# A batched matrix product on one core: the first y ahead of the first x in the load queue

## The chip, the cores and the metric

The kernel runs on one core of a Trainium2 chip. The metric is the device time of one execution in microseconds (us). The time before is the median of eight runs.

## The reference

`x` is (32, 256, 512) and `y` is (32, 512, 384), both float32. For each of the 32 batches the result is the matrix product of the two, (256, 384), float32:

```
def reference(x, y):
    return np.einsum('bij,bjk->bik', x, y).astype(np.float32)
```

16.8 MB of x and 25.2 MB of y are read, and 12.6 MB of output are written. Each is moved once.

## The kernel before

The work goes in pairs of batches (`G = 2`), 16 pairs in all (`U`). x is loaded for four batches at once (`Q = 4`) by `load_x(q)` at L66: one transfer of 2048 KB, in which each of the 128 partitions gets one contiguous run of 16 KB. y is loaded one batch at a time at L81: a transfer of 768 KB, 6 KB for each partition. A pair's output is stored by one transfer of 768 KB at L150. All these transfers are issued by SyncE, on one queue.

TensorE contracts over partitions, so x has to be turned around first. `transpose(q, half)` does it with 16 TensorE transposes of 128 x 128 in float32 (L99) into PSUM tiles `t_ps`, four transposes to a tile. VectorE (L105) and ScalarE (L107) take turns in copying these to `xt_sb` as float16. `round_y(u)` casts a pair's y to float16 in eight pieces of 128 x 384, four on ScalarE (L116) and four on VectorE (L118). `multiply(u)` runs 32 matmuls (L130) into four PSUM tiles `o_ps`; `collect(u)` copies these to `o_sb` on ScalarE (L143) and VectorE (L145); `store(u)` issues the output's transfer.

Nothing is left to a scheduler: `keep` fixes the order in which each engine meets its instructions to the order of the program. Two pairs are loaded ahead (`ahead`), and then the loop over `s` loads pair `s + 2`, collects pair `s - 2`, multiplies pair `s - 1`, rounds pair `s`, transposes a half of the next x where one is due, and stores pair `s - 2`. In step 0 both halves of the first x are transposed ahead of the first rounding. `load(u)` puts the next x in front of its own two y for every second pair, so that the queue of SyncE begins with x 0, two y of pair 0, x 1, two y of pair 1, two y of pair 2, x 2. The first store stands on that queue behind the loads of pairs 0 to 4.

There are three buffers for x, five pairs of y, two of rounded y, two of turned x and five of output. PSUM is shared half and half by transposes (four tiles) and matmuls (four tiles).

Of the kernel before, what the change touches and what calls it, by code (L numbers as in the profile page):

```python
# [1 line left out]

# [5 lines left out]


MM_DT = mybir.dt.float16  # L10
F32 = mybir.dt.float32
P = 128


Q = 4
G = 2

LAG = 4


@with_exitstack
def kernel(
    ctx: ExitStack,
    tc: tile.TileContext,
    x: bass.AP,
    y: bass.AP,
    out: bass.AP,
):
    nc = tc.nc

    B, I, J = x.shape
    _, _, K = y.shape


    M = P // G
    NE = I // M
    NJ = J // P

    PQ = P // Q
    R = I // PQ
    H = R // NE
    U = B // G

    const_pool = ctx.enter_context(tc.tile_pool(name="const", bufs=1))
    x_pool = ctx.enter_context(tc.tile_pool(name="x_pool", bufs=3))
    y_pool = ctx.enter_context(tc.tile_pool(name="y_pool", bufs=5))
    yr_pool = ctx.enter_context(tc.tile_pool(name="yr_pool", bufs=2))
    xt_pool = ctx.enter_context(tc.tile_pool(name="xt_pool", bufs=2))  # L50
    o_pool = ctx.enter_context(tc.tile_pool(name="o_pool", bufs=5))
    tpsum_pool = ctx.enter_context(tc.tile_pool(name="tpsum", bufs=4, space=bass.MemoryType.PSUM))
    opsum_pool = ctx.enter_context(tc.tile_pool(name="opsum", bufs=4, space=bass.MemoryType.PSUM))


    keep = tc.keep_in_program_order

    identity = const_pool.tile([P, P], F32)
    make_identity(nc, identity)

    x_of, y_of, yr_of, xt_of, ps_of, o_of = {}, {}, {}, {}, {}, {}

    def load_x(q):
        x_of[q] = x_pool.tile([P, R, J], F32, name="x_sb")
        keep(
            nc.sync.dma_start(  # L66
                out=x_of[q],
                in_=x[q * Q : (q + 1) * Q].rearrange("g (p r) j -> (g p) r j", r=R),
            )
        )  # L70

    def load(u):

        if u == 0:
            load_x(0)
        if (u + 1) * G % Q == 0 and u + 1 < U:
            load_x((u + 1) * G // Q)
        y_of[u] = y_pool.tile([P, G, NJ, K], F32, name="y_sb")
        for g in range(G):
            keep(  # L80
                nc.sync.dma_start(  # L81
                    out=y_of[u][:, g],
                    in_=y[u * G + g].rearrange("(q t) k -> q t k", q=P),
                )
            )

    def transpose(q, half):

        x_sb = x_of[q]
        if half == 0:  # L90
            xt_of[q] = xt_pool.tile([P, NJ, NE, Q * PQ, H], MM_DT, name="xt_sb")
        n = 0
        for t in range(half * NJ // 2, (half + 1) * NJ // 2):
            for e in range(0, NE, 2):
                t_ps = tpsum_pool.tile([P, 2, H, Q * PQ], F32, name="t_ps")
                for f in range(2):
                    for h in range(H):
                        keep(
                            nc.tensor.transpose(  # L99
                                t_ps[:, f, h], x_sb[:, h * NE + e + f, t::NJ], identity  # L100
                            )
                        )
                dst = xt_of[q][:, t, e : e + 2].rearrange("c f p h -> c f h p")
                if n % 2 == 0:
                    keep(nc.vector.tensor_copy(dst, t_ps))  # L105
                else:
                    keep(nc.scalar.copy(dst, t_ps))  # L107
                n += 1

    def round_y(u):  # L110
        y_sb = y_of.pop(u)
        yr_of[u] = yr_pool.tile([P, G, NJ, K], MM_DT, name="y_r")
        for g in range(G):
            for t in range(NJ):
                if t % 2 == 0:
                    keep(nc.scalar.copy(yr_of[u][:, g, t], y_sb[:, g, t]))  # L116
                else:
                    keep(nc.vector.tensor_copy(yr_of[u][:, g, t], y_sb[:, g, t]))  # L118

    def multiply(u):  # L120
        xt_sb, y_r = xt_of[u * G // Q], yr_of.pop(u)
        ps_of[u] = []
        for e in range(NE):
            o_ps = opsum_pool.tile([P, K], F32, name="o_ps")
            ps_of[u].append(o_ps)
            for t in range(NJ):
                for g in range(G):
                    a = (u * G + g) % Q
                    keep(
                        nc.tensor.matmul(  # L130
                            o_ps[g * M : (g + 1) * M],
                            xt_sb[:, t, e, a * PQ : (a + 1) * PQ].rearrange("c p h -> c (p h)"),
                            y_r[:, g, t],
                            start=(t == 0),
                            stop=(t == NJ - 1),
                        )
                    )

    def collect(u):
        o_of[u] = o_pool.tile([P, NE, K], F32, name="o_sb")  # L140
        for e in range(NE):
            if e % 2 == 0:
                keep(nc.scalar.copy(o_of[u][:, e], ps_of[u][e]))  # L143
            else:
                keep(nc.vector.tensor_copy(o_of[u][:, e], ps_of[u][e]))  # L145
        del ps_of[u]

    def store(u):
        keep(
            nc.sync.dma_start(  # L150
                out=out[u * G : (u + 1) * G].rearrange("g (m e) k -> (g m) e k", e=NE),
                in_=o_of.pop(u),
            )
        )


    ahead = LAG - 2
    for u in range(ahead):
        load(u)
    for s in range(U + 2):  # L160
        if s + ahead < U:
            load(s + ahead)
        if s == 0:
            transpose(0, 0)
            transpose(0, 1)
        if s >= 2:
            collect(s - 2)
        if 1 <= s <= U:
            multiply(s - 1)
        if s < U:  # L170
            round_y(s)
        for half in range(2):
            q = (s + 1 - half) * G // Q
            if (s + 1 - half) * G % Q == 0 and 0 < q < B // Q:
                transpose(q, half)
        if s >= 2:
            store(s - 2)


# [1 line left out]
_INS = ['x', 'y']  # L181
_OUTS = [((32, 256, 384), 'float32')]


# [23 lines left out]
```

## Time and profile before

| What | Value |
|---|---|
| median of 8 runs | 136.1 us (135.97 to 136.31) |
| the profiled execution | 136.31 us |
| its span, first to last instruction | 134.4 us |
| TensorE matmul busy | 91.9 us (68%) |
| VectorE, ScalarE busy | 56.5 us (42%), 64.0 us (48%) |
| DMA queue of the kernel | 54.53 MB, 97.7% of the 16 engines' span |
| mean rate | 406 GB/s over the span |
| mean granted TensorE clock | 0.909 |

The span is shorter than the execution by 1.9 us, which lie around it. Busy times are sums over an engine's instructions. A line such as "y_r L116 <- DMA y_sb" in the waits means that the instruction of line 116 could start when that transfer had landed. "SPq" is the queue of SyncE: an instruction that waits there holds up all that is behind it. In the timeline, what stands in square brackets is the idle time ahead of an instruction and what ended it. An answer by windows has, for each stretch of time, the busy time of each engine, the granted TensorE clock, the busy share of the DMA engines and the rate that they reached.

### The profile page before, as it was taken

To read this page: it belongs to the slowest core of one execution; us is meant where nothing else is said; L and a number is where in the kernel's file an instruction comes from. 1 tells how busy PE (TensorE), PEld (TensorE's weight loads), DVE (VectorE), ACT (ScalarE), POOL (GpSimd) and SP (SyncE) were. 2 spreads that over 40 slices of the span, in tenths; PEclk is the share of its full clock that TensorE was granted. 3 is DMA by queue.
4 is the path that set the end of the run, shared out by engine and by line. 5 is a ranking of instruction groups with operands and counts; after the bars stand their busy time and mean duration, and the time that the engine had idled before them with its cause. 6 is when DMAs were issued, how large, how long until landed. Compare 5 with 4: busy or idle time off the path is not lost.

```text
span 134.4 us, 1968 instructions
## 1 busy us (share of the span) xinstructions
PE 91.9 (68%) x768; PEld 75.2 (56%) x768; DVE 56.5 (42%) x128; ACT 64.0 (48%) x129; POOL 0.7 (1%) x6
## 2 busy tenths in 40 slices
PE   0049599688697925979089780997929793597920
PEld 0049568576586824768067660776726683466810
DVE  0014614744747056261644418324273704628520
ACT  3004744935766067361754428425385505737710
POOL 2000000000000000000000000000000000000000
PEclk9999968999999997799977997569986999869999
DMA  5999999999999999999999999999999999999993
GB/s 107 429 402 451 409 417 417 459 386 426 409 451 410 411 422 419 461 388 425 418 436 450 395 422 422 449 427 397 419 426 455 403 413 428 420 428 419 414 375 145
DMA packets 8073, 54.65 MB, mean 406 GB/s; under 512 B 896, under 2 KB 896, under 8 KB 7040
## 3 DMA queue, kind: packets, MB, share of 16 engines
q1 hardware_dynamic: 8064, 54.53, 97.7%
q8 instruction: 6, 0.10, 0.3%
q14 instruction: 3, 0.02, 0.0%
HBM read 41.94 MB, written 12.58 MB: 406 GB/s over the span
## 4 chain that ended last, share of the span: by engine, by line
DMA 78%; PE 13%; ACT 4%; DVE 0%; issue 0%
DMA y_sb<-in_y_dram 40%; DMA x_sb<-in_x_dram 38%; PE o_ps L130 11%; ACT xt_sb L107 2%; PE t_ps L99 2%; ACT y_r L116 1%; ACT o_sb L143 1%; DVE o_sb L145 0%
## 5 line engine op out<-in xcount | busy, mean ns | idle before, releaser
L130 PE MATMUL o_ps<-y_r,xt_sb 128*64 128x384 f16 x512 | 55.5, 379 | 28.1 <-ACT o_sb L143 20.3
L130 PEld LDWEIGHTS <-xt_sb 128*64 128x64 f16 x512 | 40.6, 126 | 39.3 <-issue 22.0
L116 ACT CAST y_r<-y_sb 128x384 f16<-128x384 f32 x64 | 29.4, 513 | 36.3 <-DMA y_sb<-in_y_dram 36.3
L99 PE MATMUL t_ps<-identity,x_sb 128*128 128x128 f32 x256 | 37.4, 304 | 8.7 <-DMA x_sb<-in_x_dram 8.6
L99 PEld LDWEIGHTS t_ps<-identity,x_sb 128*128 128x128 f32 x256 | 34.6, 212 | 13.8 <-issue 13.3
L118 DVE CAST y_r<-y_sb 128x384 f16<-128x384 f32 x64 | 19.9, 355 | 43.8 <-DMA y_sb<-in_y_dram 43.8
L107 ACT CAST xt_sb<-t_ps 128x512 f16<-128x512 f32 x32 | 22.6, 732 | 26.2 <-PE t_ps L99 26.2
L105 DVE CAST xt_sb<-t_ps 128x512 f16<-128x512 f32 x32 | 22.7, 730 | 26.9 <-PE t_ps L99 26.9
L145 DVE COPY o_sb<-o_ps 128x384 f32<-128x384 f32 x32 | 16.3, 544 | 2.1 <-PE o_ps L130 2.1
L143 ACT COPY o_sb<-o_ps 128x384 f32<-128x384 f32 x32 | 14.0, 493 | 1.3 <-PE o_ps L130 1.3
L107 ACT ACT_TABLE_LOAD x1 | 1.3, 1283 | 0.7 <-PEq L192 0.7
masks.py:199 POOL TENSOR_SCALAR_AFFINE_SELECT identity<-identity 128x128 f32<-128x128 f32 x1 | 0.3, 294 | 0.1
masks.py:197 POOL MEMSET identity<- 128x128 f32 x1 | 0.2, 205 | 0.3 <-POOLq L192 0.3
L192 POOL MEMSET const-bfloat16-1.0<- 128x1 bf16 x1 | 0.1, 102 | 0.0
L192 POOL MEMSET const-uint8-127<- 128x1 uint8 x1 | 0.1, 102 | 0.0
L192 POOL MEMSET const-float32-0.0<- 128x1 f32 x1 | 0.1, 99 | 0.2 <-issue 0.2
L192 POOL MEMSET const-float32-1.0<- 128x1 f32 x1 | 0.1, 99 | 0.0
## 6 DMA issues: line engine op xcount, KB each, us to landing
y_sb<-in_y_dram SPq DMA_DIRECT2D x32, 768.0 KB, 17.9
x_sb<-in_x_dram SPq DMA_DIRECT2D x8, 2048.0 KB, 20.8
out_dram<-o_sb SPq DMA_DIRECT2D x16, 768.0 KB, 17.8
```

What stands on the lines that cost most here:

```text
L99: nc.tensor.transpose(t_ps[:, f, h], x_sb[:, h * NE + e + f, t::NJ], identity)
L105: keep(nc.vector.tensor_copy(dst, t_ps))
L107: keep(nc.scalar.copy(dst, t_ps))
L116: keep(nc.scalar.copy(yr_of[u][:, g, t], y_sb[:, g, t]))
L118: keep(nc.vector.tensor_copy(yr_of[u][:, g, t], y_sb[:, g, t]))
L130: nc.tensor.matmul(o_ps[g * M : (g + 1) * M], xt_sb[:, t, e, a * PQ : (a + 1) * PQ].rearrange("c p h -> c (p h)"), y_r[:, g, t], start=(t ...
L143: keep(nc.scalar.copy(o_of[u][:, e], ps_of[u][e]))
L145: keep(nc.vector.tensor_copy(o_of[u][:, e], ps_of[u][e]))
L192: nc = _bacc.Bacc("TRN2", target_bir_lowering=False, num_devices=1)
```

## The change

The first load of x is issued after the first y instead of ahead of it. The queue begins with y 0, x 0, y 1, x 1, and goes on as before. The tiles, the buffers, the loop and the order on the compute engines stay.

```
     def load(u):
 
-        if u == 0:
-            load_x(0)
         if (u + 1) * G % Q == 0 and u + 1 < U:
             load_x((u + 1) * G // Q)
         y_of[u] = y_pool.tile([P, G, NJ, K], F32, name="y_sb")
...
                     in_=y[u * G + g].rearrange("(q t) k -> q t k", q=P),
                 )
             )
+            if u == 0 and g == 0:
+                load_x(0)
```

## The prediction

> **What bounds the kernel now.** I read the page first: section 1 for the engines, section 2 for how steady the load is, section 4 for the chain. Then the waits of SyncE's queue, because the change only touches the order on that queue, and the timeline of the first 40 us.
>
> ```profile
> PE 91.9 (68%) x768; PEld 75.2 (56%) x768; DVE 56.5 (42%) x128; ACT 64.0 (48%) x129; POOL 0.7 (1%) x6
> ...
> DMA  5999999999999999999999999999999999999993
> ...
> q1 hardware_dynamic: 8064, 54.53, 97.7%
> ...
> DMA 78%; PE 13%; ACT 4%; DVE 0%; issue 0%
> ```
>
> No compute engine is busy for more than 68% of the span. The DMA row is full from the second slice to the last but one, and the kernel's one queue fills the 16 DMA engines for 97.7% of the span. 54.53 MB have to move, whatever their order, and the chain is DMA for 78%. The two places where the DMA row is below 9 are the first slice (start-up) and the last (drain). So an edit pays only if it changes these ends, or empties the queue between them.
>
> The second view is the waits of SyncE's queue, up to 45 us. Columns: line, what it waited for, us in total, times, longest.
>
> ```profile
> SPq L81 <- DMA x_sb<-in_x_dram: 8.8, 2, 4.6
> SPq L81 <- DMA y_sb<-in_y_dram: 7.6, 5, 1.5
> SPq L150 <- DVE o_sb L145: 5.7, 1, 5.7
> SPq L66 <- DMA x_sb<-in_x_dram: 3.5, 1, 3.5
> ```
>
> Loads wait for earlier loads to land: the first eight loads are issued by 4.9 us, and the ninth (the third x) at 8.44, when the first has landed. Each later one follows the landing of the one eight places ahead (10.29, 12.18, 17.08, 18.96 us). Up to eight transfers are thus in flight. Only one wait here hangs on compute: the first store, 5.7 us, for VectorE's copy of the first outputs.
>
> The third view is the timeline (start, duration, instruction, idle before and its releaser).
>
> ```profile
> 8.56 6.55 PE L99 MATMUL t_ps<-identity,x_sb 128*128 128x128 f32 x32 [8.56 <-DMA x_sb<-in_x_dram]
> ...
> 15.29 1.15 DVE L118 CAST y_r<-y_sb 128x384 f16<-128x384 f32 x4
> 15.74 1.74 ACT L116 CAST y_r<-y_sb 128x384 f16<-128x384 f32 x4
> ...
> 25.29 0.35 SPq L150 DMA_DIRECT2D out_dram<-o_sb  x1
> ```
>
> TensorE's first work waits for the first x, at 8.43 us. The first casts of y stand behind the eight copies of the transposes in the order of VectorE and ScalarE, and run at 15.29 and 15.74 without a wait.
>
> **What the Trainium skill says.** "DMA: Bandwidth & Descriptors", section "Queues, rings and completion order", says that each DMA engine takes a queue's descriptors in ring order. The trace agrees: the first x and the first two y are landed at 8.43, 10.29 and 12.18, one after another. So the exchange of two transfers moves only the landing of these two. Of the clock, "TensorE: Matmul & The Clock Gate", Part 1, says that an idle window of about 3.4 us halves it, and that the windows are not tied to the kernel's start. The trace has 0.50 at 18 to 20 us and again at 118 to 120.
>
> **The change, part by part.** It adds and removes no instruction: SyncE issues the same loads, with the first y (768 KB) ahead of the first x (2048 KB). From the third load on the order is the same.
>
> *The y that moves forward.* It moved behind x from 8.43 to 10.29. In front, it has the start-up to itself: 236 GB/s from 1.5 to 4.0 us (0.59 MB), the other 0.20 MB at 418 GB/s in 0.47 us, then some 0.8 us from last byte to landing (2.10 MB of x had moved by about 7.6 us, and its landing was seen at 8.43). So it lands near 5.3 us, 5 us earlier. I cost that gain at nothing: the casts at 15.29 and 15.74 are behind the transposes' copies and do not move ahead of them. The issue itself (0.42 us for a y in this stretch, 0.37 for the first x) lies beside the start-up, and seven more issues follow before the first landing. The third x now waits for the y and is issued some 3 us earlier, into a queue already 7 deep: worth nothing.
>
> *The x that moves back.* One y of queue time: 10.28 - 8.43 = 1.85 us. The 32 transposes go from 8.56 to 10.4, their copies end at 17.7 instead of 15.9, the first matmul moves from 16.29 to 18.1, the second batch's casts (18.97 for its first half) are caught between: ScalarE is done with the first four at about 19.3 and has to be ready for the second half at 20.85. TensorE stays late: first pair's matmuls end near 23.5 instead of 21.65, and the first outputs' copy is done at 26.8 instead of 24.96. The first store goes from 25.29 to 27.1.
>
> *Does the delay reach the queue?* Before that store the ten y and three x loads are issued, the last at 18.96. At 27.1 the third x (landing 30.84 by the next landing wait of the queue), two y pairs behind it, five transfers and 2.10 + 4 x 0.79 = 5.2 MB, are still to move or moving: at 418 GB/s that is 12.5 us at 25.3 us, or over 10 us at 27.1. So the queue doesn't run dry. The two loads behind the store went out at 25.74 and 26.18, and the next at about 31 when that x landed; that one doesn't move. The second store (32.63) waits for the landing of a y; its data, copied by 31.4, would come at 33.2, so it goes out 0.8 us late with seven in flight. ScalarE was idle 1.32 and 0.88 us before the casts at 32.66 and 34.46, so its casts there are on time again; TensorE's chain of transposes, copies and matmuls can carry the rest to about 49 us, where its chain waits for a y again (the wait ends at 49.25). Price on the path: 0.
>
> *Start-up.* This the old trace doesn't show for a y. With x in front, 0.59 MB took 2.5 us where 418 GB/s needs 1.41: a loss of 1.1 us. A y's rows are 6 KB for each partition, an x's 16 KB. Bounds: at best the whole 1.1 us is saved (shorter rows get going at once); at worst the y goes wholly at 236 GB/s, 3.33 us instead of 2.97, 0.36 us lost. I take 0, since the DMA engines are already 0.91 busy in this stretch, which looks like slow first packets for whatever comes first, and since y behind x showed no second start-up (434 GB/s from 8 to 12 us).
>
> *The end.* The last store is issued at 129.4 and the DMA share is 0.78 between 129 and 130 (320 GB/s), so the last pair's compute leaves about 0.2 us of the DMA engines unused. That compute starts with y landings after 113 us and doesn't see the head. It moves only with the loads, one for one.
>
> The sum: 0 on the profiled execution, which is 136.31 us (span 134.4 and 1.9 around it). It lies 0.2 us above the median of the eight runs, so I set 136.1 against their median, 136.1. A measurement of this kernel can tell about 0.2% (0.27 us) from no change.
>
> **The rivals.**
>
> *A, the likeliest: nothing reaches the end.* 136.1 us, between 135.85 and 136.35. For it: a full DMA row, and 10 us of queued transfers when the late store comes.
>
> *B, faster: start-up of the DMA engines.* With y in front, half or more of the 1.1 us is saved, and every later landing moves with it: 135.5, at best 135.0. For it: the low 236 GB/s, and the gap can only be repaired there. Against: the low rate may be a matter of the first microseconds and not of what is first.
>
> *C, slower: the late start of the transposes is passed on.* The place is the first store, which heads a queue that can't be overtaken. It decides from the point at which the store comes after the loads ahead of it have landed; that is 12.5 us later than now, and the delay is 1.85. If it did, all 1.85 us would be on the path: 137.95. A milder form is a start-up that is worse with 6 KB rows, or a tail that meets a halved clock more often: 136.4 to 136.8.
>
> *D: the change doesn't do what it says.* If an earlier y let its casts start before x has landed, the first matmul would come sooner. It would give nothing at the end either (136.1), and the order of the two engines speaks against it.
>
> **How the numbers follow.** A with D 0.58, B 0.24, C 0.18 (0.04 for its full price, 0.14 for the milder form). A lies within 0.2%, so the chances are these. The range reaches half way into B and to the milder C: 135.5 to 136.7; the likeliest case alone has 135.85 to 136.35.
>
> **What would show it.** Right: TensorE's first wait for x ends near 10.3 us instead of 8.56; the first casts of y move from 15.29 to about 17.1 on VectorE; the first store is issued near 27; the load after it still goes out near 31; the DMA row reads 9 from the second slice on, and the last store is issued near 129.4. Wrong: a rate from 1.5 to 4.0 us that is not near 236 GB/s, with landings at 31 us and 113 us moved by the same amount (B or its opposite); a digit below 9 in the DMA row between 20 and 45 us (C); casts of y ahead of 10 us (D).

## The result, and the profile after

The changed kernel is slower: 136.83 us (136.66 to 137.09, 11 runs) against 136.15 us for the kernel before (135.83 to 136.57, 32 runs), a ratio of 1.005, 95% interval 1.004 to 1.006. The forecast was 136.1.

The first profile is of an execution of 136.34 us, quicker than any other run of this kernel; a second one, taken with the experiments (after_2, the same code), is of 137.10 us, and stands for the median better. Both are read here, each time beside the two profiles of the kernel before (136.31 and 135.96 us).

The page of the first one: DMA share in 40 slices, rate in the same slices, the kernel's queue.

```profile
DMA  4999999999999999999999999999999999999993
GB/s 148 461 391 466 389 424 430 452 385 415 309 450 408 416 426 426 445 408 418 423 433 444 402 424 424 441 428 401 422 426 452 416 405 424 420 429 422 416 393 136
...
q1 hardware_dynamic: 8064, 54.53, 97.7%
```

The rate of the kernel before, from its page:

```profile
GB/s 107 429 402 451 409 417 417 459 386 426 409 451 410 411 422 419 461 388 425 418 436 450 395 422 422 449 427 397 419 426 455 403 413 428 420 428 419 414 375 145
```

The DMA row is as full as before, and the queue's share is 97.7% again. By these two lines nothing has happened. The rate tells it: the first slice has 148 GB/s instead of 107, and the eleventh, 33.6 to 37.0 us, has 309 instead of 409. The second profile has 303 there. A DMA engine that is slow at moving is as "busy" as one at full rate.

By windows (stretch, length, busy us of PE, PEld, DVE, ACT, POOL, clock, DMA share, GB/s) of the changed kernel, first profile, then second, then of before, first and second:

```profile
1.50:4.00 2.50, 0.00 (x0) 0.00 (x0) 0.00 (x0) 0.51 (x1) 0.00 (x0) 1.00 0.94 334
...
33.00:37.00 4.00, 2.08 (x22) 1.90 (x21) 3.20 (x8) 3.21 (x8) 0.00 (x0) 1.00 1.01 323
```

```profile
1.50:4.00 2.50, 0.00 (x0) 0.00 (x0) 0.00 (x0) 0.51 (x1) 0.00 (x0) 1.00 0.99 360
33.00:37.00 4.00, 2.46 (x22) 2.30 (x22) 2.85 (x7) 3.12 (x7) 0.00 (x0) 1.00 1.01 307
```

```profile
1.50:4.00 2.50, 0.00 (x0) 0.00 (x0) 0.00 (x0) 0.51 (x1) 0.00 (x0) 1.00 0.91 236
33.00:37.00 4.00, 2.65 (x25) 2.25 (x21) 2.84 (x8) 3.12 (x8) 0.00 (x0) 1.00 1.01 412
```

```profile
1.50:4.00 2.50, 0.00 (x0) 0.00 (x0) 0.00 (x0) 0.52 (x1) 0.00 (x0) 1.00 0.92 256
33.00:37.00 4.00, 1.21 (x12) 1.12 (x12) 2.85 (x8) 3.13 (x8) 0.00 (x0) 1.00 1.02 415
```

Two things have changed. The start moves (334 - 236) x 2.5 = 0.25 MB more by 4.0 us, some 0.6 us at 418 GB/s. From 33 to 37 us the rate is 323 or 307 where 412 to 415 were had: (413 - 323) / 413 x 4 = 0.9 us lost in the first profile, 1.0 us in the second.

In bytes most of the gain is still there at 33 us: over the first 33 us both profiles of the changed kernel have a mean of 396 GB/s, those of the kernel before 390 and 389, which makes 0.2 MB or 0.5 us. Over the first 37 us it is 388 and 386 against 392 in both, so 0.3 to 0.5 us have been lost by then on top of the whole gain.

A landing gains less than the mean rate. ScalarE's wait for the second y of pair 1 ends at 20.65 and 20.63 us, against 20.85 and 20.97 before: 0.2 to 0.3 us. The Trainium skill, "DMA: Bandwidth & Descriptors", section "Why a DMA increments its semaphore by 16 and not by 1", says that the engines of a transfer finish independently and that only the full count means all data landed; so the latest of the 16 engines counts. The trace agrees: it has a completion mark for each engine, and for this y the middle ones of the 16 are at 19.9 us in both profiles, 0.5 to 0.6 us earlier than before (20.5 and 20.4), while the last is only 0.2 to 0.3 us earlier.

The same marks show which transfer is slow. For the middle engines the second y of pair 4, the last load ahead of the first store, comes 2.6 and 2.7 us after the y ahead of it, where the kernel before has 1.9 in both profiles; the store itself then follows after 1.9 us. The packets agree: those of 6 KB that began between 35 and 36 us took 455 ns at the median in the first profile, those of 30 to 33 us 238 ns.

Where the loss is final is read off SyncE's timeline, in the second profile of the changed kernel:

```profile
24.91 0.35 SPq L150 DMA_DIRECT2D out_dram<-o_sb  x1
...
32.44 0.34 SPq L150 DMA_DIRECT2D out_dram<-o_sb  x1
...
39.49 0.34 SPq L150 DMA_DIRECT2D out_dram<-o_sb  x1
...
112.32 18.09 SPq L150 DMA_DIRECT2D out_dram<-o_sb  x5
```

and in the first of the kernel before:

```profile
32.63 0.34 SPq L150 DMA_DIRECT2D out_dram<-o_sb  x1
...
38.81 0.34 SPq L150 DMA_DIRECT2D out_dram<-o_sb  x1
...
111.54 18.16 SPq L150 DMA_DIRECT2D out_dram<-o_sb  x5
```

The second store goes out when the first y of pair 3 has landed: at 32.63 us in both profiles before, at 31.97 and 32.44 after, still 0.2 to 0.7 us early. The third goes out when the second y of pair 4 has landed: at 38.81 and 38.38 us before, at 39.10 and 39.49 after. From there to the burst of the last five stores it is 72.73 and 72.86 us before, 72.62 and 72.83 after. So by these landings the whole difference is there by 39 us, and the rest carries it to the end: spans of 134.4 and 134.2 against 134.6 and 135.2 us.

### The profile page after: what moved, and what is told of

Same layout as the page of the kernel before. It is cut to its first block, busy times and chain, and to the rows that moved or that the text cites. A ratio compares the mean times of both kernels' runs of the same rounds, so it can differ in the third digit from the quotient of the medians.

```text
span 134.6 us, 1968 instructions
## 1 busy us (share of the span) xinstructions
PE 91.4 (68%) x768; PEld 74.2 (55%) x768; DVE 56.5 (42%) x128; ACT 64.1 (48%) x129; POOL 0.7 (1%) x6
## 3 DMA queue, kind: packets, MB, share of 16 engines
q1 hardware_dynamic: 8064, 54.53, 97.7%
## 4 chain that ended last, share of the span: by engine, by line
DMA 82%; PE 9%; ACT 2%; SPq 2%; issue 0%; DVE 0%
DMA y_sb<-in_y_dram 53%; DMA x_sb<-in_x_dram 15%; DMA out_dram<-o_sb 13%; PE o_ps L130 7%; PE t_ps L99 2%; ACT xt_sb L107 1%; SPq L66 1%; ACT y_r L116 1%; SPq L79 1%; DVE o_sb L145 0%; ACT o_sb L143 0%; SPq L150 0%
## 5 line engine op out<-in xcount | busy, mean ns | idle before, releaser
L130 PE MATMUL o_ps<-y_r,xt_sb 128*64 128x384 f16 x512 | 56.3, 383 | 27.0 <-ACT o_sb L143 19.3
L99 PE MATMUL t_ps<-identity,x_sb 128*128 128x128 f32 x256 | 36.1, 297 | 10.2 <-DMA x_sb<-in_x_dram 10.2
L99 PEld LDWEIGHTS t_ps<-identity,x_sb 128*128 128x128 f32 x256 | 33.3, 211 | 15.3 <-issue 15.3
L107 ACT CAST xt_sb<-t_ps 128x512 f16<-128x512 f32 x32 | 22.6, 732 | 27.1 <-PE t_ps L99 27.0
```

The source lines that it names most:

```text
L99: nc.tensor.transpose(t_ps[:, f, h], x_sb[:, h * NE + e + f, t::NJ], identity)
L130: nc.tensor.matmul(o_ps[g * M : (g + 1) * M], xt_sb[:, t, e, a * PQ : (a + 1) * PQ].rearrange("c p h -> c (p h)"), y_r[:, g, t], start=(t ...
```

## The experiments

Two readings of the loss were set against each other: that the later x delays the compute and so the queue (theory C of the prediction), and that the loads themselves run slowly at one place (R). Later ones ask what belongs to that place. The table has the median time, its ratio to the kernel before measured on the same chip with the 95% interval, and the rate in three windows of the profile. Each kernel has one profile, which need not be of a typical run: that of store_late is of its quickest (135.52 us), that of swap_quads of its slowest (137.63).

| kernel | us | ratio | 1.5 to 4 us | 17 to 21 us | 33 to 37 us |
|---|---|---|---|---|---|
| before_2 | 136.08 | 0.9995 (0.9984 to 1.0007) | 256 | 419 | 415 |
| after_2 | 137.06 | 1.0059 (1.0039 to 1.0080) | 360 | 424 | 307 |
| yyx | 136.96 | 1.0050 (1.0039 to 1.0062) | 317 | 412 | 307 |
| late_before | 136.10 | 0.9998 (0.9983 to 1.0013) | 236 | 421 | 413 |
| swap_quads | 136.83 | 1.0065 (1.0044 to 1.0086) | 302 | 426 | 352 |
| touch_y9 | 137.20 | 1.0087 (1.0064 to 1.0109) | 319 | 416 | 346 |
| touch_x | 137.35 | 1.0106 (1.0081 to 1.0131) | 238 | 426 | 358 |
| split_x | 136.65 | 1.0050 (1.0030 to 1.0069) | 262 | 419 | 386 |
| split_part | 140.96 | 1.0351 (1.0330 to 1.0371) | 210 | 418 | 391 |
| hold_x2 | 137.28 | 1.0074 (1.0049 to 1.0098) | 324 | 426 | 327 |
| touch_out | 136.92 | 1.0053 (1.0033 to 1.0074) | 299 | 417 | 330 |
| touch_same | 137.15 | 1.0058 (1.0037 to 1.0079) | 321 | 411 | 332 |
| store_late | 136.35 | 1.0013 (1.0001 to 1.0025) | 296 | 429 | 445 |
| first_late | 136.49 | 1.0013 (0.9998 to 1.0027) | 315 | 427 | 450 |
| big_early | 139.04 | 1.0223 (1.0185 to 1.0260) | 295 | 289 | 422 |
| before_big_early | 138.85 | 1.0211 (1.0163 to 1.0259) | 236 | 358 | 422 |
| desync | 137.26 | 1.0075 (1.0055 to 1.0095) | 292 | 403 | 418 |
| desync_late | 139.32 | 1.0232 (1.0198 to 1.0266) | 278 | 421 | 195 |

### Again, and the compute's delay

after_2 and before_2 are the two kernels unchanged.

> The changed kernel once more, for a second profile. Theory R (slow reads): in the first profile the loads landed early (0.2 us at 24 us, 0.8 at 30 to 34), and then lost it all and more between 34 and 39 us, where the rate fell to 309 GB/s in a slice that had 409 before. If this belongs to the order of the loads, it is there again: a loss of 0.8 us or more in the stretch of 33 to 40 us, larger in this profile if its execution is nearer to 136.8. Theory S (a single event): the slice reads near 410 GB/s and the time is lost elsewhere. Time 136.8 in both.

> The kernel before once more, for a second profile: 136.15 us. Theory R expects no slice under 375 GB/s between the second and the last but one; theory S that such a slice can turn up here too, somewhere.

The slow stretch is there again after the change (307 GB/s) and not before (415). R holds, and a single event is out.

yyx puts the second y ahead of x as well:

```
-            if u == 0 and g == 0:
+            if u == 0 and g == 1:
                 load_x(0)
```

> Both y of the first pair ahead of the first x; all else as in the changed kernel. If the loss comes from the late start of the transposes (theory C, delay passed on), it doubles, as x lands near 12.0 us instead of 10.1: about 137.5. Theory R: the loads' order from the fourth on is as before, so the same loss at the same place, 136.8; if the loss depends on when the first output is ready against the loads, it changes, in a direction that this theory doesn't give.

TensorE's first work waits until 12.11 us for x (10.22 in the changed kernel, 8.56 before), and the first store goes out at 26.12 us. The time is that of the changed kernel, with the same 307 GB/s. So 1.9 us more of delay costs nothing, and C falls in its full form. It fits that the first store of the changed kernel (24.05 and 24.91 us) isn't later than that of the kernel before (25.29 and 23.86).

late_before keeps the old order of loads and puts the first y's casts ahead of the transposes' copies:

```
         if s == 0:
+            round_y(0, [0])
             transpose(0, 0)
...
         if s < U:
-            round_y(s)
+            round_y(s, [1] if s == 0 else range(G))
```

> The kernel before with its order of loads, but the casts of the first y put ahead of the transposes' copies on ScalarE and VectorE, so that the copies wait for the y (10.3 us) and the compute starts about 1.3 us late. Theory C: 136.8, as in the changed kernel, since only the late compute counts. Theory R: 136.15, since the loads' order is that of before.

The time is that of before. But it is a weaker test than meant: the first copy waits until 11.03 us instead of 9.70, and then half of the casts are out of the way, so that the first store goes out at 23.93 us, earlier than before (25.29).

### Place in memory, first touches, the early ninth issue

The slow loads are those ahead of the first store, the second y of pair 4 above all (batch 9). swap_quads exchanges batches 8 to 11 with 12 to 15 in x, y and output:

```
+    at = [0, 1, 3, 2, 4, 5, 6, 7]
...
+                in_=x[at[q] * Q : (at[q] + 1) * Q]...
```

> The changed kernel, with the third and the fourth group of four batches exchanged: the places in the queue hold batches 12 to 15 where 8 to 11 were, and the other way round. In both profiles of the changed kernel the load of batch 9, the thirteenth on the queue, is slow on all engines (some 0.8 us at 34 to 36 us). Theory A (the place in memory): the loss moves with batch 9, to some 13 us later, near 50 us, and the slice near 35 us is back at 410 GB/s. Theory T (the place in the queue or in time): the loss stays near 34 to 36 us. Time 136.8 in both.

352 GB/s from 33 to 37 us, 422 from 46 to 50 us: the stretch is milder, but stays at its place in the queue. Theory A, for the place in memory, is out.

touch_y9 and touch_x add one small load (128 rows of 512 B) of batch 9 behind the second pair, or of x ahead of everything:

```
+    touched = const_pool.tile([P, 128], F32)
+    keep(nc.sync.dma_start(out=touched, in_=y[9].rearrange("(q t) k -> q (t k)", q=P)[:, 0:128]))
```

> The changed kernel, with one more small load (128 rows of 512 B of batch 9, never used) behind the first two pairs' loads. Theory A, with a first touch that costs: the cost is paid by the small load, most of it beside the other transfers in flight, and the slice near 35 us is at 410 GB/s; with the better start-up kept, 135.7 to 136.1. Theory T: no change of the slow stretch, 136.8 to 137.0 with the extra load's issue and its place among the eight in flight.

> The changed kernel, with one more small load (128 rows of 512 B of the first x, never used) ahead of the first y, so that x is touched first as in the kernel before. Theory A, if the loss depends on which tensor is touched first: the slow stretch near 35 us goes, and the time is 136.1 plus up to 0.5 for the small load's own time at the head (136.1 to 136.6). Theory T, if it depends on the order of the large loads: the slow stretch stays, 136.9 to 137.3.

Neither removes it (346 and 358 GB/s), and both times (137.20 and 137.35 us) are above what either theory gave.

hold_x2 holds back the third x, which the change lets out at 5.2 us:

```
+    held = x_pool.tile([P, R, J], F32, name="x_sb")
+    nc.gpsimd.memset(held[:, 0, 0:8], 0.0)
...
+                    if q == 0 and half == 0 and n == 1:
+                        keep(nc.scalar.copy(seen, held[:, 0, 0:8]))
```

> The changed kernel with the third x's load held until ScalarE's first copy of the transposes is done (about 12 us; in the changed kernel it goes out at 5.2, in the kernel before at 8.4), by a buffer that is first given to a tile of which ScalarE reads eight columns there. Theory E (the early ninth issue, into a full queue, is to blame): no slow stretch at 34 to 36, and 135.7 to 136.0 with the better start-up. Otherwise unchanged: 136.8.

The load goes out at 12.93 us, and the stretch is there, 327 GB/s, at 137.28 us. The early issue is not the cause.

### The first store

store_late issues every store two steps later:

```
-        if s >= 2:
-            store(s - 2)
+        if s >= 4:
+            store(s - 4)
```

> The changed kernel with every store issued two steps later, so that the first one stands on the queue behind the loads of pair 6 instead of pair 4. Theory W (the slow stretch belongs to the first store, the queue's first writes): it moves with the store, from the fifth pair's second y to the loads just ahead of the new place, some 12 us later. Theory Q (it belongs to that place among the loads): it stays at 34 to 36 us. The time of the whole isn't comparable, as the last stores come later: 137 to 141.

```profile
1.50:4.00 2.50, 0.00 (x0) 0.00 (x0) 0.00 (x0) 0.51 (x1) 0.00 (x0) 1.00 0.88 296
...
33.00:37.00 4.00, 2.84 (x26) 2.51 (x24) 3.16 (x8) 3.14 (x7) 0.00 (x0) 1.00 1.07 445
46.00:50.00 4.00, 2.45 (x27) 2.20 (x27) 3.31 (x8) 3.68 (x8) 0.00 (x0) 1.00 1.03 411
```

The stretch at 33 to 37 us is gone (445 GB/s), with a quick start (296 GB/s). Ahead of the store's new place only a little is lost: 411 GB/s from 46 to 50 us. So it belongs to the first store, and in this profile it shrinks as it moves. The time is 136.35 us, not the 137 to 141 expected, and 0.7 us under after_2, with the last stores later than in the changed kernel.

touch_out and touch_same write a small block (128 rows of 512 B) early, to the last pair's or the first pair's rows of the output:

```
+    keep(nc.sync.dma_start(out=out[B - G : B].rearrange("g (m e) k -> (g m) e k", e=NE)[:, 0, 0:P], in_=identity))
```

> The changed kernel with one small store (128 rows of 512 B, to rows of the output that the last store overwrites) behind the first two pairs' loads. Theory W, if the queue's first write to the output costs: the slow stretch near 35 us goes or shrinks, and shows some 10 to 24 us earlier, at the small store. Time 136.8 if the cost only moves, 136.0 if it is hidden. Theory Q: slow stretch unchanged, 136.8 to 137.2.

> The changed kernel with one small store (128 rows of 512 B) to the rows of the first pair's output, which the first store overwrites, behind the first two pairs' loads. If a first access to this part of the output costs: the slow stretch at 34 to 36 us falls from 0.8 us of all engines to under 0.2, and the time to 136.2. If not: 136.9 as with the small store to the last pair's rows.

330 and 332 GB/s: neither a first write as such, if it is small, nor a first access to these rows is the cause.

big_early puts a whole store of 768 KB there:

```
+    blank = const_pool.tile([P, NE, K], F32)
+    nc.gpsimd.memset(blank, 0.0)
...
+    keep(nc.sync.dma_start(out=out[B - G : B].rearrange("g (m e) k -> (g m) e k", e=NE), in_=blank))
```

> The changed kernel with a whole store of 768 KB (zeros, to the last pair's rows, overwritten at the end) behind the first two pairs' loads, so that the queue's first large write is near 20 to 25 us. If the first large write is what costs: a slow stretch just ahead of it, at 18 to 23 us, and none at 36 to 38; time 136.85 + 1.9 (0.79 MB at 418 GB/s) = 138.7. If the cost belongs to the place or the time: none at 18 to 23, one at 36 to 38, the same time.

```profile
1.50:4.00 2.50, 0.00 (x0) 0.00 (x0) 0.00 (x0) 0.52 (x1) 1.05 (x2) 1.00 0.87 295
17.00:21.00 4.00, 3.14 (x33) 2.19 (x32) 1.12 (x4) 2.46 (x6) 0.00 (x0) 1.00 0.98 289
33.00:37.00 4.00, 2.32 (x19) 2.10 (x17) 0.73 (x3) 1.03 (x3) 0.00 (x0) 1.00 1.01 422
```

The slow stretch has gone with it: 289 GB/s from 17 to 21 us, where the changed kernel has 426, and 422 at 33 to 37. The outputs' own first store, whose turn now comes later by the added bytes and the loss, costs nothing: 419 GB/s from 36 to 40 us. 139.04 us is 2.9 us over the kernel before on this chip (136.17): 1.9 us for the bytes and some 1.0 us more, the loss of the changed kernel. With store_late it shows that the slow stretch goes with the queue's first whole store, and lies ahead of it.

before_big_early is the same edit on the kernel before.

> The kernel before, x in front, with the same whole store of 768 KB of zeros behind the first two pairs' loads (to the last pair's rows, overwritten at the end). If the cost is paid once, at the slow start (0.9 us): no slow stretch at 17 to 22 us, and 136.15 + 1.9 = 138.05. If an early large store costs whatever the start was: a slow stretch there as with y in front (1.2 us), and 139.0.

```profile
17.00:21.00 4.00, 3.94 (x39) 3.36 (x34) 0.63 (x2) 0.93 (x2) 0.00 (x0) 1.00 1.00 358
33.00:37.00 4.00, 2.17 (x16) 2.12 (x17) 0.71 (x3) 1.01 (x3) 0.00 (x0) 1.00 1.02 422
```

358 GB/s, 0.6 us lost in that window where big_early loses 1.3 (against the 424 that the kernel before has there). So x in front doesn't make the queue immune: an early store costs there too, though half as much, after a slow start that has been paid already. A cost paid once, at the start or at the store, would have left nothing here. The time, 138.85 us, is nearer to the 139.0 of the other expectation, but two of the four runs are near 138.3, the profiled one among them, and two near 139.5.

### What the start has to do with it

split_x loads the first x in two transfers with rows of 8 KB, split_part in two of 64 partitions with rows of 16 KB, both ahead of y:

```
+        n = 2 if q == 0 else 1
+        for i in range(n):
+            rows = slice(i * R // n, (i + 1) * R // n)
...
+                    out=x_of[q][:, rows],
```

> The kernel before, x first, with the first x loaded by two transfers of 1024 KB, 8 KB a row. Theory of row size at the start-up: the loss of the first 4 us falls from 0.9 us towards the 0.4 of the changed kernel, and with no slow stretch near 35 us the time is 135.6 to 135.9. If the start-up's loss belongs to what is first touched and not to the row size: 136.1 as before.

> The kernel before, x first, with the first x loaded by two transfers of 64 partitions each, its rows of 16 KB kept. Theory L (long rows first): what spares the kernel before the slow stretch near 35 us is that its queue starts with rows of 16 KB; then this has the start-up of before (0.5 MB at 4.0 us), no slow stretch, and 136.1. If it is the count or the size of the first transfers that matters, the slow stretch is there and the time 136.5 to 136.8.

split_x starts a little quicker (262 against 236 and 256 GB/s) and has a milder slow stretch (386), with the order of tensors that was thought safe: 136.65 us. Neither of the two times expected came, and by the rate only 0.3 us are lost in that stretch, where the time is 0.6 us over that of the kernel before: the rest is not accounted for. In split_part the loads of 64 partitions run at 210 and 205 GB/s (1.5 to 4 and 4 to 8 us), so everything comes some 5 us later, and its time (140.96 us) can't be used. The place in the queue of the first store lies there at about 36 to 44 us, and the rate is 418 GB/s at 36 to 40 and 431 at 38 to 44: here the first store costs nothing.

A slow start alone isn't what spares a kernel. touch_x, with a small load and then y in front, starts as slowly as the kernel before (238 GB/s from 1.5 to 4 us), has no lead at 33 us (a mean of 389 GB/s, as before), and still has the slow stretch (358).

desync adds a load of 8 partitions behind the first y, desync_late one of twice the row behind the fourth pair:

```
+                some = const_pool.tile([8, 4 * K * 2], F32)
+                keep(nc.sync.dma_start(out=some, in_=y[0, 0 : 64].rearrange("(q t) k -> q (t k)", q=8)))
```

(The expectation of desync says 24 KB a row and 0.9 us. As built it was 12 KB, half of that.)

> The changed kernel with one small load more behind the first y, of 8 partitions with 24 KB each, so that 8 of the 16 DMA engines get 0.9 us of extra work and stand apart from the other 8. If the slow stretch needs engines that arrive together: it falls to under 0.4 us; the time is 136.3 to 137.0, as the 8 later engines set the end with 0.9 us more. If not: slow stretch 0.7 to 1.1, and 137.5 to 137.8.

> The changed kernel with one small load (8 partitions, 24 KB each, never used) behind the fourth pair's loads, so that some of the DMA engines are 0.9 us behind the others when the first store comes, after a start as quick as in the changed kernel. If the slow stretch needs engines that arrive together: none, and a time of 136.8 to 137.2 from the extra load. If it is a cost paid once: it is there, ahead of the store or already behind the small load, 0.7 to 1.1 us, and 137.3 to 137.9.

In desync nothing is lost at the first store (418 GB/s), but the loads behind the small one are slow: 313 GB/s from 4 to 8 us, where after_2 has 418. Its time (137.26 us) lies between the two expected. In desync_late the small load itself is so costly (195 GB/s at a share of 0.84) that what the store adds can't be seen. Whether it matters how closely the engines arrive stays open.

### A version meant to keep the gain

first_late delays the first store by two steps and lets the next ones catch up:

```
-        if s >= 2:
-            store(s - 2)
+        if s >= 4:
+            for u in {4: [0], 5: [1, 2], 6: [3, 4]}.get(s, [s - 2]):
+                store(u)
```

> The changed kernel with the first store two steps later and the next four catching up, so that from the seventh step on the stores stand where they were. If the slow stretch shrinks as with all stores late (0.2 us instead of 0.9), the start-up's gain is kept: 135.7 to 136.1. If the loss only moves: 136.6 to 136.9.

450 GB/s from 33 to 37 us, and 136.49 us over 22 runs (135.62 to 137.01): 0.3 to 0.6 us better than the changed kernel, but not better than the kernel before, and in neither of the two ranges expected. In its profile, of a run of 136.75 us, the slow stretch is gone and time is lost at the end instead: 337 GB/s from 125 to 128 us, where the kernel before has 407 and 415. So the slow stretch isn't all that separates the kernels; what slows that end stays open. No version here beats the kernel before.

## Why the prediction was wrong

*What bounds the kernel* was right, but read too simply. The full DMA row was taken for a fixed rate, so that a fixed list of transfers had to take a fixed time. The row is as full after the change, and the rate in one stretch is a quarter lower.

*The step that failed* is in "what the Trainium skill says": "So the exchange of two transfers moves only the landing of these two." The landings move through the whole queue: 0.2 to 0.3 us early at 20.6 us, and 0.3 to 1.1 us late at 39 us. In its place stands a term that the sum doesn't have: the loads ahead of the first whole store, +0.9 to +1.0 us by their rate. The prediction priced the store only by when its data are ready, not by what it does to the loads ahead of it.

*Start-up.* I took 0 within a gain of 1.1 and a loss of 0.36. It was a gain, some 0.6 us by the rate (334 and 360 GB/s against 236 and 256), 0.2 to 0.7 us at the landings. Rival B's mechanism is real, and was outweighed. At 39 us the landings are 0.3 to 1.1 us late, 0.7 in the mean of the four pairs of profiles, which is the difference of the medians (136.83 - 136.15 = 0.68). By the bytes moved in 37 us it is only 0.3 to 0.5 us: two profiles of each kernel give the size no more closely than this.

*The x that moves back.* TensorE's wait ends at 10.22 us, as forecast (10.3). The first casts of y come at 15.75 and 16.59 us and not near 17.1, since the transposes took 5.35 and 6.28 us instead of 6.55. The 31 matmuls behind the first took 2.85 us in both profiles, where the forecast kept the 4.53 us of the halved clock; the second profile of the kernel before has 2.85 too, so that clock belonged to one execution and not to the order of the loads. The first store came at 24.05 and 24.91 us and not at 27.1, and the second early instead of 0.8 us late. "Price on the path: 0" was right, and yyx shows that it would have been with 1.9 us more.

*The y that moves forward.* It landed when the third x was issued, 5.23 us (forecast near 5.3), and the early landing of this y brought nothing, as costed. hold_x2 agrees on the early third x.

*The rivals.* C had the right sign and the right place, the first store, with another mechanism: not a store that comes too late for its queue, but one that, when its turn nears, slows the loads ahead of it. Its milder form named a worse start-up and a halved clock at the end; neither was seen. That its 136.4 to 136.8 us comes so near the 136.83 measured is luck. None of the rivals had this.

*What is open.* Why the kernel before loses nothing at its own first store (412 and 415 GB/s), while it does at an earlier one, so what in the order of the first two loads brings the loss about; and by what means a store slows the loads in front of it. The runs show when it happens and not how.

## What to carry to other kernels

In a kernel bound by transfers, read the rate by slices and not the busy share: the share was full in both kernels while a quarter of the rate was missing. Here the queue's start and its first store were the places where the rate was not the steady one, and a change at the head moved both. Compare landings at a few fixed transfers along the queue to find where a difference becomes final.

## What the runs showed of the hardware

With y in front, the first whole store of 768 KB on the queue took the rate down to 289 to 323 GB/s over 4 us, ahead of its own turn (after, after_2, big_early); the later stores in the same kernels didn't. Two loads of 64 partitions, one behind the other, ran at 205 GB/s from 4 to 8 us (split_part), where one of 128 partitions has 418, and one of 8 partitions, with the first store close behind, brought the whole queue to 195 GB/s for 4 us (desync_late). And the order of the first two loads changed the start: 0.84 MB instead of 0.59 MB by 4.0 us with rows of 6 KB in front of rows of 16 KB; a load of 512 B rows ahead of these took the start back to 238 GB/s (touch_x), so the length of the first rows alone doesn't set it.
